# Hybrid encoder step on one core: key transposes queued behind a later token tile, index query weight loaded later

## Chip, cores, metric

The kernel runs on one core of one Trainium2 chip. The metric is the device time of one execution in microseconds, the median of several runs. Times inside the execution are counted from the first instruction of the profiled execution.

## What is computed

One inference step of a one-layer encoder, for 1024 frames of a new stream (eight token tiles of 128 rows) and for 8 x 16 frames of running streams (a ninth token tile). Cut to the part that matters here:

```
h    = rmsnorm(x, norm_mix)              # x: 1152 x 1024
proj = h @ w_in                          # 1024 x 2376, split into:
xr, gate, q, k, v, qi, ki, wi = parts
ki   = rope(ki, pos)                     # index keys, 64 wide, one per token
qi   = rope(qi.reshape(T, 8, 64), pos)   # index queries, 512 columns of w_in
score = sum_h relu(qi_h . ki) * wi_h     # picks 256 keys per query
...                                      # RG-LRU, attention over the picked keys, output, SwiGLU
```

Products are made from pairs of float32r numbers (a rounded part, "hi", and the rest, "lo"), three matmuls for one product.

## The kernel before

The program is written as Python generators, called streams, that emit instructions and yield the time after which they want to go on. `run` (line 93) steps them by a clock of its own, made of planner costs (0.137 us for a projection matmul, 0.109 us for a transpose, and fixed costs of the other engines). It keeps at most `width` main streams open and opens the next when one has ended; `side` streams such as the weight loader are stepped when their own time has come. The order of emission is the priority with which a scheduler then fills each engine's queue at build time; it may bring an instruction forward past earlier ones on its engine. In the first stage TensorE's order in the trace is that of emission, while ScalarE, VectorE and the DMA queue show instructions that were brought forward.

The first stage has nine main streams `norm_kv(i)` (line 555), one for each token tile, with `W_NORM = 3` open at once. One of them, for tile i:

- loads x(i) (512 KB, line 561; the pool has four such buffers);
- `norm_T` (line 466): ScalarE squares and sums a row, VectorE makes the inverse root and scales x(i); then TensorE makes eight 128 x 128 transposes in two groups of four (line 217), and each group is split by ScalarE (hi, 128 x 512) and VectorE (lo, 128 x 512) into the tile `h`;
- 24 matmuls of 328 columns against the weight `wk` give keys, values, index keys and index weights of this tile (line 207);
- ScalarE copies the result to `kv` and squares two 64-column parts of it; the rotary embedding makes the index key `kr` from `kv` (`rope`, VectorE, with two products on POOL from tile 3 on); `kr` goes out by DMA (line 591);
- `stack_keys` (line 596): one transpose of `kr` on TensorE, two ScalarE copies and two VectorE subtractions into the stacked index keys `ki1` and `ki2`.

With three streams open in step, emission comes in groups of three: the x transposes of three tiles, the 72 matmuls of the three, the three `kr` transposes, then the next three tiles. Tile 0 goes first and alone, tiles 1 to 3 follow as a group, then 4 to 6, then 7 and 8. Start times `X_T` hold tiles 0 to 2 apart.

The `loader` (line 420) is a side stream. Its first job is `load_512` (line 608): four DMAs of 512 KB into two `raw` buffers bring the 512 columns of the index query weight; each is split into two weight tiles by a ScalarE copy (hi) and a POOL subtraction (lo, 128 x 512). With `LOAD_AT = 0` the loader begins at once. The next stage, `index` (line 622), starts with tile 8 and needs this weight, `h` and later `ki1`, `ki2`.

After that come the LRU group, attention, the output projection and the feed-forward part, which ends the kernel.

Of the kernel before, what the change touches and what calls it, by code (L numbers as in the profile page):

```python
# [21 lines left out]
NT = 9  # L22
# [59 lines left out]
class Kernel:  # L82
# [131 lines left out]
    def tr(self, out, in_):  # L214
        self.pe += 0.109
        n = in_.shape[0]
        self.nc.tensor.transpose(out, in_, self.ident[0:n, 0:n])  # L217

    def ps(self, n=512, name="ps"):
        return self.psum.tile([128, 512], F32, tag="b", name=name)  # L220
# [45 lines left out]
    def build(self, upto=99):  # L266
# [14 lines left out]
        self.hblk = ctx.enter_context(tc.tile_pool(name="h", bufs=6, side=L))  # L281
        tka_p = pool(tka, "tka", L)
        ki_p = pool(kist, "ki", L)
        self.wused, self.W, self.locks, self.n_norm = 0, {}, set(), 0

        self.ident = self.const.tile([128, 128], F32, name="ident")
        self.eps = self.const.tile([128, 1], F32, name="eps")
# [59 lines left out]
        with tc.tile_pool(name="woa", bufs=2, side=R) as tp:  # L347
            self.phase = 3
            kr, qr = self.k_rope(tp), self.q_norm(tp)
# [55 lines left out]
    LRU_HE = ('pool', 'pool', 'pool', 'pool', 'pool', 'pool', 'pool', 'pool')  # L405
    Q_HE = 'pool'
    W_NORM = 3
    LOAD_AT = 0
    WK_LO = ('dve', 'dve', 'dve', 'dve')
    W_IDX = 4  # L410
    LRU_C = 7
# [8 lines left out]
    def loader(self):  # L420
# [6 lines left out]
        jobs += [(("wb", q, c), 2, lambda n, q=q, c=c: self.load_wb(q, c, n)) for q in range(2) for c in (0, 2)]  # L427
        while self.n_norm < self.LOAD_AT:
            yield 1.0
# [125 lines left out]
    def norm_kv(self, i, tp, g, wk):  # L555
        nc, I, O = self.nc, self.I, self.O
        self.n_norm += 1
        x = self.x.pop(i, None)
        if x is None:
            x = tp.tile([128, D], F32, tag="x", name="x", bufs=4)  # L560
            nc.sync.dma_start(x, self.x_src(i))
        if i < len(self.X_T):
            yield from self.until(self.X_T[i])
        yield from self.norm_T(x, x, g, self.h[i // 3], (i % 3) * 128, tp)
        t = self.ready
        yield 0.0
        yield from self.until(max(t, self.WK_T))
        pk = self.ps()
        for d in range(ND):
            self.mm3(pk[:, :328], self.h_lhs(i, d, 0), self.h_lhs(i, d, 1), wk[:, d, 0, :], wk[:, d, 1, :],  # L570
                     d == 0, d == ND - 1)
        self.begin()
        kv = tp.tile([128, 328], F32, tag="kv", name="kv")
        nc.scalar.activation(kv, pk[:, :328], AF.Copy)
        tab = self.tables(tp, i)
        kr = tp.tile([128, 64], F32, tag="kr", name="kr")
        self.rope(kr[:, None, :], kv[:, None, 256:320], tab, 1, tp, "dve", self.KR_E[i > 2], "dve")
        t = self.end() + self.KV_LAT
        nc.gpsimd.tensor_scalar(self.kn[:, i, :], kv[:, 0:128], 1.0, 0.0, op0=ALU.mult, op1=ALU.add)
        sq = tp.tile([128, 128], F32, tag="sq", name="sq")  # L580
        for a in range(2):
            nc.scalar.activation(sq[:, a * 64:a * 64 + 64], kv[:, a * 64:a * 64 + 64], AF.Square, scale=0.125,
                                 accum_out=self.kss[:, i, a:a + 1])
        self.hi(self.vhl[:, i, 0, :], kv[:, 128:256], "pool")
        self.lo(self.vhl[:, i, 1, :], kv[:, 128:256], self.vhl[:, i, 0, :])
        vo = O["v_p"][0, i * 128:(i + 1) * 128] if i < NP else O["v_s"].rearrange("b t k d -> (b t) k d")
        nc.sync.dma_start(vo.rearrange("t k d -> t (k d)"), kv[:, 128:256])
        nc.gpsimd.tensor_scalar(self.wi[:, i, :], kv[:, 320:328], 8.0 ** -0.5 * 64.0 ** -0.5, 0.0,
                                op0=ALU.mult, op1=ALU.add)
        ko = O["ki_p"][0, i * 128:(i + 1) * 128] if i < NP else O["ki_s"].rearrange("b t d -> (b t) d")  # L590
        nc.sync.dma_start(ko, kr)
        yield 0.0
        yield from self.until(t)
        self.stack_keys(kr, self.ki1[:, i * 128:(i + 1) * 128], self.ki2[:, i * 128:(i + 1) * 128])

    def stack_keys(self, src, k1, k2):

# [442 lines left out]
    def lru_main(self, n, c, lp):  # L1040
# [62 lines left out]
        def gates(t):  # L1103
            xc = xcs[t]
            if not t:
                trs.append(lp.tile([128, 1152], F32, tag="tr", name="tr", bufs=2))
            tr, ti, tt = trs[0][:, 384 * t:384 * t + 384], third("ti"), third("tt")
            G.append((tr, ti, tt))
            for k, dst in ((0, tr), (1, ti)):
                pg = self.ps()  # L1110
                self.mm4(pg[:, :384], bd[:, k, :], xc, True, True)
                S.activation(dst, pg[:, :384], AF.Tanh, scale=0.5, bias=hb[:, c, k:k + 1])
            S.activation(tt, tr, AF.Tanh, scale=sp2[:, c:c + 1], bias=sp2[:, c:c + 1])
            V.scalar_tensor_tensor(ti, ti, 1.0, xc, op0=ALU.add, op1=ALU.mult)
            self.c_free += 1
# [637 lines left out]
```

## Time and profile before

| what | value |
|---|---|
| median of 3 runs | 1537.71 us (1537.52 to 1539.65) |
| the profiled execution's own time | 1536.94 us |
| its span, first to last instruction | 1535.1 us |
| mean granted TensorE clock | 0.98 of full |
| first index matmul on TensorE | 72.59 us |
| TensorE busy | 1467.9 us (96%) |

In rows of a timeline the first number is the start, the second the time from the start of the first to the end of the last instruction of a merged row, then engine, line, operation, output and input tiles, shapes and count; the bracket is the engine's idle time before the row and what ended it. PE is TensorE, DVE VectorE, ACT ScalarE, SPq the queue of the sync engine that issues the DMAs. PEclk is the granted clock, 1.00 for 2.4 GHz and 0.50 for 1.2 GHz.

### The profile page before, as it was taken

The page shows a single profiled execution, that of the slowest core. Times are in us where ns is not written, and L with a number is a line of the kernel's source. Part 1 is how long each engine was busy: PE and PEld are TensorE (multiplying, and loading weights), DVE is VectorE, ACT ScalarE, POOL GpSimd, SP SyncE. Part 2 cuts the span into 40 slices and gives each one's busy share as a digit, 9 for nine tenths or more (in the row PEclk, how much of TensorE's full clock was granted, in tenths as well). Part 3 has the DMA queues.
Part 4 walks back from the last instruction along what each step waited for, and adds up shares of the span by engine and source line. Part 5 has one row for each costly group of instructions (what it writes and reads, how often), then busy time and mean ns, then how long its engine had stood idle before and what let it go on. Part 6 is the DMA issues. An engine that isn't in the chain of part 4 may idle for free.

```text
span 1535.1 us, 20876 instructions
## 1 busy us (share of the span) xinstructions
PE 1467.9 (96%) x7786; PEld 1307.5 (85%) x7786; DVE 865.2 (56%) x1904; ACT 619.2 (40%) x1481; POOL 269.7 (18%) x425
## 2 busy tenths in 40 slices
PE   6889899889997999999999999999999999999998
PEld 6877688778745788889999998989898989898987
DVE  7556899899967988777233333342424242515233
ACT  5447988977415877745202020202121212111100
POOL 4214234333774544300000000000000000000000
PEclk8999899999998999999999999999999999999999
DMA  7201110010401002122102020202021111111003
GB/s 241 58 18 30 48 38 22 12 31 32 176 28 28 1 15 69 28 69 82 56 0 83 0 83 1 83 5 79 18 66 28 56 42 42 50 34 56 28 1 123
DMA packets 95093, 75.24 MB, mean 49 GB/s; under 512 B 13380, under 2 KB 85828, under 8 KB 94992
## 3 DMA queue, kind: packets, MB, share of 16 engines
q1 hardware_dynamic: 94992, 73.91, 15.9%
q8 instruction: 61, 1.00, 0.3%
q14 instruction: 40, 0.33, 0.1%
HBM read 67.62 MB, written 6.27 MB: 48 GB/s over the span
## 4 chain that ended last, share of the span: by engine, by line
PE 72%; DVE 13%; ACT 6%; issue 5%; POOL 2%; DMA 1%; SPq 0%; ACTq 0%; DVEq 0%; POOLq 0%
PE ps L207 66%; DVE junk L66 4%; PE ps L217 3%; ACT jk L66 3%; PE ps L212 3%; DVE tk_cand L66 2%; DVE tr L66 1%; ACT L66 1%; POOL rp L66 1%; DVE ti L66 1%; DVE qn L66 1%; ACT tr L66 1%; DVE m L66 1%; ACT relu L66 1%; DVE s L66 1%
## 5 line engine op out<-in xcount | busy, mean ns | idle before, releaser
L207 PE MATMUL ps<-hf,w 128*128 128x384 f32 x2556 | 453.1, 334 | 0.0
L207 PEld LDWEIGHTS ps<-hf,w 128*128 128x128 f32 x2556 | 444.2, 188 | 0.7
L207 PE MATMUL ps<-w,a 128*128 128x512 f32 x999 | 238.4, 389 | 0.0
L66 DVE TENSOR_TENSOR acc<-ps,acc 128x512 f32<-128x512 f32 x234 | 161.0, 690 | 118.2 <-PE ps L207 117.4
L207 PEld LDWEIGHTS ps<-w,a 128*128 128x128 f32 x999 | 187.3, 188 | 38.5
L66 ACT ACTIVATE w<-raw 128x512 fp32r<-128x512 f32 x124 | 75.2, 628 | 295.7 <-PE ps L207 219.2
L66 DVE TENSOR_TENSOR sg<-ps,sg 128x384 f32<-128x384 f32 x66 | 36.8, 557 | 276.7 <-PE ps L207 276.1
L66 ACT ACTIVATE a<-sg 128x384 fp32r<-128x384 f32 x66 | 34.5, 523 | 219.4 <-DVE sg L66 219.4
L66 DVE TENSOR_TENSOR w<-raw,w 128x512 fp32r<-128x512 f32 x116 | 76.9, 688 | 81.7 <-ACT w L66 81.5
L207 PE MATMUL ps<-hf,rest 128*128 128x384 f32 x612 | 114.3, 334 | 0.0
L66 ACT ACTIVATE jk<-s,tk_cand 128x384 bf16<-128x384 f32 (+3 forms) x128 | 99.5, 777 | 32.4 <-DVE tk_cand L66 29.7
L207 PEld LDWEIGHTS ps<-hf,rest 128*128 128x128 f32 x612 | 106.9, 188 | 0.2
L207 PE MATMUL ps<-h,w 128*128 128x384 f32 x576 | 106.7, 342 | 0.0
L207 PEld LDWEIGHTS ps<-h,w 128*128 128x128 f32 x576 | 100.4, 188 | 3.9 <-ACT relu L66 0.2
L207 PE MATMUL ps<-w,h 128*128 128x256 f32 (+1 forms) x600 | 97.7, 320 | 0.0
L207 PEld LDWEIGHTS ps<-w,h 128*128 128x128 f32 x600 | 85.1, 194 | 6.5
L66 ACT ACTIVATE sg<-ps 128x384 f32<-128x384 f32 x66 | 32.0, 486 | 119.7 <-PE ps L207 119.7
L212 PE MATMUL ps<-wa,yF 128*128 128x512 f32 x144 | 63.4, 593 | 2.4 <-DVE k L66 1.5
L66 POOL TENSOR_SCALAR m<-m,mx 128x128 f32<-128x128 f32 (+7 forms) x64 | 51.7, 814 | 54.1 <-DVE mx L66 45.2
L212 PEld LDWEIGHTS ps<-wa,yF 128*128 128x128 f32 x144 | 26.5, 190 | 35.5 <-issue 31.9
L66 ACT ACTIVATE m<-m,mx 128x128 f32<-128x128 f32 (+7 forms) x64 | 49.3, 771 | 16.4 <-DVE mx L66 16.0
L207 PE MATMUL ps<-k,qeo 128*128 128x384 f32 (+5 forms) x192 | 51.9, 383 | 3.7 <-DVE qeo L66 2.9
(266 smaller groups left out, 2139.8 us busy)
## 6 DMA issues: line engine op xcount, KB each, us to landing
raw<-in_w_ffn_in_dram SPq DMA_DIRECT2D x44, 512.0 KB
raw<-in_w_ffn_out_dram SPq DMA_DIRECT2D x22, 512.0 KB
raw<-in_w_in_dram SPq DMA_DIRECT2D x16, 512.0 KB
out_dram<-acc SPq DMA_DIRECT2D x9, 512.0 KB
x<-in_x_prompt_dram SPq DMA_DIRECT2D x8, 512.0 KB
acc<-in_x_prompt_dram SPq DMA_DIRECT2D x8, 512.0 KB
tab<-in_rope_dram SPq DMA_DIRECT2D x43, 64.0 KB
wa<-in_w_out_dram SPq DMA_DIRECT2D x4, 512.0 KB
```

The costliest lines, as they stand in the source:

```text
L66: return f(*args, **kw)
L207: self.nc.tensor.matmul(out, lhsT, rhs, start=start, stop=stop)
L212: self.nc.tensor.matmul(out, lhsT, rhs, start=start, stop=stop)
L217: self.nc.tensor.transpose(out, in_, self.ident[0:n, 0:n])
```

## The change

Each `norm_kv(i)` notes the last x transpose of its tile. Before `stack_keys`, stream i waits until the x transposes of tile i + 2 (at most tile 8) have been emitted, and the `kr` transpose gets an edge that puts it behind the last of them in TensorE's queue. The loader begins when the fourth `norm_kv` has begun. No instruction is added or removed.

```diff
     def tr(self, out, in_):
         self.pe += 0.109
         n = in_.shape[0]
-        self.nc.tensor.transpose(out, in_, self.ident[0:n, 0:n])
+        self.last_tr = self.nc.tensor.transpose(out, in_, self.ident[0:n, 0:n]).ins
...
-    LOAD_AT = 0
+    LOAD_AT = 4
...
         yield from self.norm_T(x, x, g, self.h[i // 3], (i % 3) * 128, tp)
+        self.xt[i] = self.last_tr
         t = self.ready
...
         yield 0.0
         yield from self.until(t)
-        self.stack_keys(kr, self.ki1[:, i * 128:(i + 1) * 128], self.ki2[:, i * 128:(i + 1) * 128])
+
+        n = min(i + 2, NT - 1)
+        while n not in self.xt:
+            yield 0.3
+        with self.tc.issue_after(self.xt[n]):
+            self.stack_keys(kr, self.ki1[:, i * 128:(i + 1) * 128], self.ki2[:, i * 128:(i + 1) * 128])
```

## Rows read from the trace of the kernel before

**Rows 1.** The page's head: span, TensorE's busy time, and the shares of the chain that ended last, by engine.

```profile
span 1535.1 us, 20876 instructions
PE 1467.9 (96%) x7786; PEld 1307.5 (85%) x7786; DVE 865.2 (56%) x1904; ACT 619.2 (40%) x1481; POOL 269.7 (18%) x425
PE 72%; DVE 13%; ACT 6%; issue 5%; POOL 2%; DMA 1%; SPq 0%; ACTq 0%; DVEq 0%; POOLq 0%
```

**Rows 2.** Busy time by stage, from the view of windows: the window, its length, busy us of TensorE, its weight loads, VectorE, ScalarE and POOL with their instruction counts, granted clock, DMA share, GB/s.

```profile
20.50:31.30 10.80, 5.42 (x25) 5.05 (x26) 9.15 (x21) 7.92 (x20) 5.51 (x8) 0.63 0.55 168
31.30:45.40 14.10, 12.42 (x77) 12.15 (x76) 13.08 (x41) 8.69 (x31) 7.55 (x15) 0.92 0.59 173
...
800.00:1535.00 735.00, 730.63 (x3865) 685.90 (x3863) 262.92 (x414) 121.03 (x225) 0.00 (x0) 1.00 0.15 46
```

**Rows 3.** TensorE's timeline through the first stage.

```profile
19.48 1.02 PE L207 MATMUL ps<-wk,h 128*128 128x328 f32 x5 [0.62 <-DVE nr L66]
24.68 0.42 PE L217 MATMUL ps<-ident,kr 128*64 128x128 f32 x1 [4.18 <-DVE kr L66]
24.89 3.62 PE L217 MATMUL ps<-ident,x 128*128 128x128 f32 x16
29.71 1.94 PE L217 MATMUL ps<-ident,x 128*128 128x128 f32 x8 [1.20 <-DVE x L66]
31.30 12.15 PE L207 MATMUL ps<-wk,h 128*128 128x328 f32 x72
...
45.34 0.27 PE L217 MATMUL ps<-ident,kr 128*64 128x128 f32 x1 [1.68 <-DVE kr L66]
45.45 2.78 PE L217 MATMUL ps<-ident,x 128*128 128x128 f32 x24
47.99 11.10 PE L207 MATMUL ps<-wk,h 128*128 128x328 f32 x72
58.93 0.38 PE L217 MATMUL ps<-ident,kr 128*64 128x128 f32 x2
60.98 0.27 PE L217 MATMUL ps<-ident,kr 128*64 128x128 f32 x1 [1.67 <-DVE kr L66]
61.09 1.91 PE L217 MATMUL ps<-ident,x 128*128 128x128 f32 x16
63.25 7.49 PE L207 MATMUL ps<-wk,h 128*128 128x328 f32 x48 [0.25 <-DVE h L66]
...
72.54 0.30 PE L217 MATMUL ps<-ident,kr 128*64 128x128 f32 x1 [1.69 <-DVE kr L66]
72.59 11.17 PE L207 MATMUL ps<-w,h 128*128 128x512 f32 x48
```

**Rows 4.** The granted clock in windows of 2 us (columns as in rows 2).

```profile
22.00:24.00 2.00, 0.00 (x0) 0.00 (x0) 2.00 (x3) 0.63 (x2) 2.00 (x2) 0.84 0.76 199
...
32.00:34.00 2.00, 2.00 (x10) 2.00 (x10) 1.97 (x4) 2.00 (x6) 1.30 (x2) 0.60 0.86 242
34.00:36.00 2.00, 2.00 (x15) 2.00 (x14) 2.00 (x4) 0.83 (x2) 1.81 (x2) 1.00 0.84 287
```

**Rows 5.** VectorE's timeline in the same stage: the subtractions for `wk`, the scaling of x, the rotary embedding of tile 0, and single rows beside POOL's work.

```profile
10.40 0.84 DVE L66 TENSOR_TENSOR wk<-yF,wk 128x656 fp32r<-128x656 f32 x1 [0.67 <-POOL wk L66]
...
16.75 2.68 DVE L66 TENSOR_TENSOR wk<-yF,wk 128x656 fp32r<-128x656 f32 x2
...
20.61 2.25 DVE L66 SCALAR_TENSOR_TENSOR x<-x,ss,gmix 128x1024 f32<-128x1024 f32 x1
22.78 1.35 DVE L66 TENSOR_TENSOR rp<-kv,tab 128x32 f32<-128x32 f32 x2
...
24.39 0.23 DVE L66 TENSOR_TENSOR kr<-kr,rp 128x64 f32<-128x64 f32 x1
...
33.30 1.28 DVE L66 TENSOR_TENSOR ss<-nr,nr 128x1 f32<-128x1 f32 x1
34.50 0.68 DVE L66 TENSOR_TENSOR h<-ps,h 128x512 fp32r<-128x512 f32 x1
...
37.71 1.28 DVE L66 SCALAR_TENSOR_TENSOR x<-x,ss,gmix 128x1024 f32<-128x1024 f32 x1
```

**Rows 6.** POOL's timeline: the first four and the last two subtractions of the index query weight.

```profile
16.94 7.04 POOL L66 TENSOR_TENSOR w<-raw,w 128x512 fp32r<-128x512 f32 x4
...
33.27 2.54 POOL L66 TENSOR_TENSOR w<-raw,w 128x512 fp32r<-128x512 f32 x2 [0.70 <-ACT w L66]
```

**Rows 7.** ScalarE's timeline: a copy of `kv` and the last of its two squares, and the h copies of tiles 7 and 8.

```profile
40.20 0.44 ACT L66 ACTIVATE kv<-ps 128x328 f32<-128x328 f32 x1 [1.64 <-issue]
...
41.08 0.19 ACT L66 ACTIVATION_READ_ACCUMULATOR sq<-kv 128x1 f32 x1
...
61.87 2.07 ACT L66 ACTIVATE h<-ps 128x512 fp32r<-128x512 f32 x4
```

**Rows 8.** The DMA queue's issues: the first two loads of the index query weight, and the load of x(3).

```profile
10.73 1.18 SPq L455 DMA_DIRECT2D raw<-in_w_in_dram  x2
...
13.07 0.34 SPq L561 DMA_DIRECT2D x<-in_x_prompt_dram  x1
```

More of the change, by code (lines that the diff above doesn't have):

```diff
@@ L283, in build @@
         ki_p = pool(kist, "ki", L)
-        self.wused, self.W, self.locks, self.n_norm = 0, {}, set(), 0
+        self.wused, self.W, self.locks, self.n_norm, self.xt = 0, {}, set(), 0, {}
         self.ident = self.const.tile([128, 128], F32, name="ident")
```

## The prediction

> **What bounds the kernel now.** The page's head comes first: TensorE is busy 96% of the span and holds 72% of the chain that ended last [rows 1]. The windows by stage then say where the missing 4% is. From 800 us to the end TensorE is busy 730.6 of 735 us at full clock [rows 2], so a microsecond won or lost in the first stage is carried to the end, as long as the stages between keep their order. The change touches only the first stage, which ends where the first index matmul starts, at 72.59 us [rows 3].
>
> In that stage the reader is to see two things. TensorE's timeline has gaps in front of index key transposes: 4.18 us before that of tile 0, 1.68 and 1.67 us before the last one of each group of three, 1.69 us before that of tile 8; one of 1.20 us stands before the x transposes of tile 3 [rows 3]. While TensorE waited for `kr` of tile 0, the scaled x(1) lay ready: its sixteen transposes with those of x(2) start at 24.89, directly behind. The second thing is the clock. TensorE falls to 1.2 GHz in the window from 22 to 24 us, in which it did nothing, and is back at 2.4 GHz only in the window after 32 us [rows 4]; the sixteen x transposes took 3.62 us at the low clock and sixteen others 1.91 us at the high one [rows 3]. VectorE is the second bound: it is busy 22.2 of the 24.9 us from 20.5 to 45.4 [rows 2], so what TensorE gives up as waiting may be asked of VectorE next.
>
> **The change, part by part.** *The key transposes.* Nothing is added; nine transposes of about 0.11 us (0.38 us for two against 0.27 us for one [rows 3]) move behind eight x transposes each. For tile 0 that fills the gap: x(1) and x(2) are transposed while `kr` of tile 0 is made. But the code does a second thing. Stream i may not end before x(i+2) is transposed, and only three streams are open, so stream i+3 cannot begin before that either. The groups of three dissolve. A norm takes longer in the planner than a tile's 24 matmuls, so from tile 3 on the emission becomes: matmuls of tile i, x transposes of tile i+1, key transpose of tile i-1, matmuls of tile i+1. The key transpose then comes a whole tile late and waits for nothing: the gaps of 1.68 and 1.67 us go. In exchange each tile's matmuls stand directly behind their own x transposes, and must wait until ScalarE and VectorE have made `h` of them. In groups of three that was hidden: 24 x transposes took until 47.99 us and the matmuls followed with no gap. The one place that shows it nearly alone is tiles 7 and 8: transposes start at 61.09, the matmuls at 63.25, so 2.16 us from start to start [rows 3].
>
> That gives the sum. Tile 0's matmuls end at 20.50 (19.48 + 1.02). Tile 1's can start at 22.7 at the earliest (20.50 + 2.16) and at 25.3 at the latest: `kr` of tile 0 arrives at 24.6 as before [rows 5], and one subtraction for `h` of 0.68 us follows it on VectorE. I take 23.9, because the chain to `kr` holds two `wk` subtractions that took 2.68 us and would take 1.68 at the 0.84 us of the first one [rows 5]; the excess lies where POOL works on the index weight [rows 6]. Tiles 1 and 2 have their transposes done by then: two times 3.70 us (11.10 / 3 [rows 3]) makes 31.3. The clock adds something: at the low clock 72 matmuls took 1.05 us more (12.15 against 11.10). Without the long idle stretch it may stay up, and I take half, 0.5: 31.8. The bounds are 0 and the 1.05. Tiles 3 to 8 cost 3.70 + 2.16 = 5.86 us each, together 35.2: 67.0. The end stays: from tile 8's last matmul (63.25 + 7.49 = 70.74) to the first index matmul at 72.59 are 1.85 us, with the wait for `kr` of tile 8, which has nothing behind which it could be put. The index stage starts at 68.8 instead of 72.59, **3.8 us earlier**.
>
> Of the 2.16 us only 1.04 are TensorE's work (0.93 for eight transposes, 2.78 / 3, and 0.11 for the key), so 1.12 us of each tile stand open. Its bounds are 1.04 (all covered) and 3.89: the ScalarE copy to `kv` and the two squares, 1.07 us from 40.20 to 41.27 [rows 7], stand in front of the h copies, which in the row of 61.87 started 0.78 us after the transposes, so some 0.45 more; and a scaling of x of 1.28 us [rows 5] can lie in front of the subtraction. I stay at 2.16, the only row of that very sequence.
>
> *The later load.* Four DMAs, eight ScalarE copies and eight POOL subtractions are the same as before, with lower priority. In the DMA queue x(3) no longer stands behind two of them (1.18 us of issue [rows 8]). That alone is worth nothing: the 1.20 us in front of x(3) were VectorE's scaling, not its landing. The weight itself is not late: its first load to its last subtraction were some 25 us before (10.73 to 35.81 [rows 6, 8]), and from 24 us on that makes 49, with the index stage at 69. If that cover were gone, each microsecond would be one.
>
> What it can bring is a free VectorE. Beside POOL's subtractions the scaling of x took 2.25 us instead of 1.28, and a one-column operation 1.28 us, while a subtraction that reads PSUM kept its 0.68 us [rows 5, 6]. The Trainium skill ("SBUF — State Buffer", section "SBUF: two separate sides") calls the port pair of VectorE and GpSimd an exclusive lock, under which a VectorE operation with two SBUF inputs is blocked for the whole GpSimd instruction; these rows agree. By that rule the load moves the blocking and removes none of it, which speaks against this half of the change: what tile 0's chain wins, the scaling and rotary embedding of tiles 1 to 4 pay.
>
> No other queue is made to wait: the ScalarE copies into `ki1` and `ki2` come a tile later, and their first readers are in the index stage.
>
> **The sum.** The profiled execution took 1536.94 us, 1.84 us around its span of 1535.1; the median of the runs is 0.77 above it. 1536.94 - 3.8 = 1533.1 for a profiled execution, 1533.9 as a median. About 0.2% (3.1 us) is what a measurement of this kernel can tell from no change.
>
> **Rivals.** *Cover found:* the scheduler brings the next tile's x transposes forward into the open 1.12 us. For it: VectorE's scalings run ahead of TensorE. Against: in the trace x(4) to x(6) stayed behind the key transpose of tile 3, though TensorE waited 1.68 us. Six times 1.12 us more, 1527.2.
>
> *VectorE takes over:* the scheduler brings the weight's loads forward anyway, since the DMA queue and POOL have room at 12 to 20 us, and POOL blocks VectorE in the same place. For it: rows 2 and the lock. Then tile 1 starts at 25.3 (1.4 lost), and one contended scaling (0.97 more) lands in front of a tile's `h`: a gain of 1.4, 1536.3.
>
> *The open evacuation is longer (slower):* from tile 3 on the matmuls wait for ScalarE's squares (0.45 us) and for part of a scaling on VectorE (0.8 of 1.28): 3.4 us from transposes to matmuls. Six times 1.24 us is 7.4, the gain of 3.8 turns to a loss of 3.6, 1541.3. It decides from 2.16 + 3.8 / 6 = 2.8 us on. For it: VectorE's 93% to 45.4 us. Against: it has room later, and has the whole of a tile's matmuls for the scaling.
>
> *It does nothing:* the emission is later than planned but the queues come out the same, 1537.7.
>
> **How the numbers follow.** Forecast 0.45, cover 0.10, VectorE 0.25, longer evacuation 0.13, nothing 0.07. The forecast's own spread, 22.7 to 25.3 for tile 1's start and the clock's 0.5 either way, leaves 0.09 of its 0.45 within 0.2%; VectorE's case gives 0.04 to faster. So faster 0.50, same 0.37, slower 0.13. The range goes from 1529.5, past the forecast's bounds and partly to the cover, to 1539.5, over the VectorE case, no change, and the near half of the loss.
>
> **What would show it.** Right: x transposes of tiles 1 and 2 ahead of the first key transpose, no `kr` wait but those of tiles 0 and 8, matmuls in 24s each about 2.2 us behind their transposes, full clock before 28 us, and the first index matmul near 69 us. Wrong: an idle time <-DVE h above 1.8 us a tile, a first stage of 72 us or more, tile 1's matmuls after 25.5, or a shift at the stage's end that the later stages give back.

## The result and the profile after

| | before | changed |
|---|---|---|
| median | 1537.71 us | 1528.2 us (1527.1 to 1534.16, 5 runs) |
| ratio to before | | 0.995 (0.9937 to 0.9963) |
| the profiled execution, its span | 1536.94, 1535.1 us | 1534.16, 1532.3 us |
| mean granted clock | 0.980 | 0.979 |
| first index matmul on TensorE | 72.59 us | 65.06 us |

The change makes the kernel faster by 0.5%, 7.7 us by the ratio (5.7 to 9.7). The forecast was 3.8 us, a median of 1533.9 in a range from 1529.5 to 1539.5. The ratio applied to the median of before gives 1530.0, inside that range; the bare median, 1528.2, lies 1.3 us below its lower end. So about twice the forecast gain came, at the edge of the range. The profiled execution of the changed kernel is the slowest of its five, so its span shows only 2.8 us of the gain; what it lost again, it lost after the first stage (last section). The first stage itself reads clearly. This is TensorE's timeline of the changed kernel, to be laid beside [rows 3]:

```profile
14.92 1.97 PE L217 MATMUL ps<-ident,x 128*128 128x128 f32 x8
16.54 2.07 PE L207 MATMUL ps<-wk,h 128*128 128x328 f32 x11
19.16 1.09 PE L217 MATMUL ps<-ident,x 128*128 128x128 f32 x8 [0.56 <-DVE x L66]
22.30 0.27 PE L217 MATMUL ps<-ident,kr 128*64 128x128 f32 x1 [2.04 <-DVE nr L66]
22.33 7.21 PE L207 MATMUL ps<-wk,h 128*128 128x328 f32 x36
...
32.08 2.06 PE L207 MATMUL ps<-wk,h 128*128 128x328 f32 x12
...
35.68 0.30 PE L217 MATMUL ps<-ident,kr 128*64 128x128 f32 x1 [0.67 <-DVE kr L66]
37.66 5.27 PE L207 MATMUL ps<-wk,h 128*128 128x328 f32 x24 [1.69 <-DVE h L66]
...
45.48 2.05 PE L207 MATMUL ps<-wk,h 128*128 128x328 f32 x12
47.37 1.03 PE L217 MATMUL ps<-ident,x 128*128 128x128 f32 x8
48.16 2.05 PE L207 MATMUL ps<-wk,h 128*128 128x328 f32 x12
50.05 0.28 PE L217 MATMUL ps<-ident,kr 128*64 128x128 f32 x1
50.08 2.06 PE L207 MATMUL ps<-wk,h 128*128 128x328 f32 x12
...
59.28 3.86 PE L207 MATMUL ps<-wk,h 128*128 128x328 f32 x24
62.98 0.27 PE L217 MATMUL ps<-ident,kr 128*64 128x128 f32 x1
65.04 0.27 PE L217 MATMUL ps<-ident,kr 128*64 128x128 f32 x1 [1.78 <-DVE kr L66]
65.06 11.17 PE L207 MATMUL ps<-w,h 128*128 128x512 f32 x48
```

The reader is to see where the x transposes stand. Those of x(1) lie inside tile 0's matmuls (14.92, between the first 13 and the last 11). From 45 us on each tile up to tile 7 is 12 matmuls, x transposes of the next tile, 12 matmuls, and the key transpose of the tile before (in tile 6 two of the eight x transposes come behind its last matmuls): tile 5 starts at 45.48, tile 6 at 50.08, tile 8 at 59.28, so 4.60 us a tile with no wait at all. The windows of this trace (columns as in rows 2) show the same: from 45.4 to 59.3 us TensorE is never idle, and before that VectorE is the fuller engine.

```profile
20.30:29.40 9.10, 7.10 (x38) 7.11 (x39) 8.88 (x21) 6.59 (x19) 6.54 (x7) 0.81 0.69 200
29.40:45.40 16.00, 13.64 (x87) 13.17 (x86) 14.57 (x45) 11.00 (x35) 10.81 (x15) 0.89 0.56 159
45.40:59.30 13.90, 13.90 (x103) 13.76 (x101) 9.20 (x23) 8.11 (x28) 4.16 (x15) 1.00 0.14 38
```

The waits that are left before 45 us, 2.04, 0.67 and 1.69 us, have POOL's subtractions of the index query weight beside them. POOL's timeline of the changed kernel, then VectorE's:

```profile
18.98 2.51 POOL L66 TENSOR_TENSOR w<-raw,w 128x512 fp32r<-128x512 f32 x2 [3.52 <-ACT w L66]
...
31.40 3.51 POOL L66 TENSOR_TENSOR w<-raw,w 128x512 fp32r<-128x512 f32 x2 [1.20 <-ACT w L66]
```

```profile
19.79 1.75 DVE L66 TENSOR_TENSOR rp<-kv,tab 128x32 f32<-128x32 f32 x2
...
31.44 2.33 DVE L66 SCALAR_TENSOR_TENSOR x<-x,ss,gmix 128x1024 f32<-128x1024 f32 x1
33.69 1.24 DVE L66 SCALAR_TENSOR_TENSOR nr<-nr,nr 128x1 f32<-128x1 f32 x1
```

The two `rp` products of tile 0's key take 1.75 us instead of the 0.38 that the same pair takes later in this trace, the scaling 2.33 instead of 1.28, one column 1.24 instead of 0.2.

### The profile page after: what moved, and what is told of

The parts are those of the page before. It is cut to its first block, busy times and chain, and to the rows that moved or that the text cites. A ratio compares the mean times of both kernels' runs of the same rounds, so it can differ in the third digit from the quotient of the medians.

```text
span 1532.3 us, 20880 instructions
## 1 busy us (share of the span) xinstructions
PE 1471.5 (96%) x7786; PEld 1309.0 (85%) x7786; DVE 867.1 (57%) x1904; ACT 618.5 (40%) x1481; POOL 266.2 (17%) x425
## 4 chain that ended last, share of the span: by engine, by line
PE 73%; DVE 11%; ACT 9%; issue 4%; POOL 3%; DMA 1%; SPq 0%; ACTq 0%; POOLq 0%; DVEq 0%
PE ps L207 66%; PE ps L217 3%; ACT jk L66 3%; DVE junk L66 3%; PE ps L212 3%; DVE tk_cand L66 2%; DVE tr L66 1%; ACT tr L66 1%; POOL rp L66 1%; ACT L66 1%; ACT relu L66 1%; DVE m L66 1%; DVE ti L66 1%; POOL s L66 0%; DMA acc<-in_x_prompt_dram 0%
## 5 line engine op out<-in xcount | busy, mean ns | idle before, releaser
L207 PE MATMUL ps<-smr,vhl 128*128 128x512 f32 x162 | 55.0, 425 | 2.4 <-ACT smr L66 1.9
```

Source lines behind the costliest of these rows:

```text
L207: self.nc.tensor.matmul(out, lhsT, rhs, start=start, stop=stop)
```

## The experiments

Two theories stood against each other at first. Theory A: the changed order of emission lets the scheduler bring the next tile's x transposes in between the matmuls of a tile, and the stage is TensorE's work alone from then on. Theory B: the later load frees VectorE, and the key transposes matter little. Of the first four kernels, two have one half of the change each, one has it whole, and one has it without the scheduler's freedom.

**e1, the later load alone.**

```diff
 (kernel before)
-    LOAD_AT = 0
+    LOAD_AT = 4
```

> The kernel before with LOAD_AT = 4 alone; key transposes as before. Theory A (the gain is TensorE's new order: the x transposes of the next tile come next in emission and are brought into the matmuls of the tile ahead): the groups of three and their gaps of about 1.7 us stay, only the head gains, first index matmul at 69 to 71 us, median 1534 to 1536. Theory B (the freed VectorE at the head is what counts): first index matmul near 66, median near 1529.

Measured: 1537.37 us beside 1538.24, ratio 0.999 (0.998 to 1.0). From 45 us on TensorE's timeline keeps the groups of three, and the waits for `kr` stay:

```profile
24.08 0.42 PE L217 MATMUL ps<-ident,kr 128*64 128x128 f32 x1 [3.24 <-DVE kr L66]
...
31.22 1.04 PE L217 MATMUL ps<-ident,x 128*128 128x128 f32 x8
...
45.11 0.27 PE L217 MATMUL ps<-ident,kr 128*64 128x128 f32 x1 [3.09 <-DVE kr L66]
45.22 2.78 PE L217 MATMUL ps<-ident,x 128*128 128x128 f32 x24
...
72.37 8.00 PE L207 MATMUL ps<-w,h 128*128 128x512 f32 x34
```

The first key waits 3.24 us instead of 4.18 [rows 3], and the key that ends the next group waits 3.09 instead of 1.68: what VectorE won in front, the group took back. By itself the load is worth 0.2 us at the first index matmul, less than theory A expected (69 to 71 us). In the first group x transposes do stand between the matmuls (31.22), in the old emission too; those of the next three tiles (45.22) stay behind the key transpose.

**e2, the key transposes alone.**

```diff
 (changed kernel)
-    LOAD_AT = 4
+    LOAD_AT = 0
```

> The changed kernel with LOAD_AT = 0: key transposes behind the token tile two later, weight load from the start. Theory A: first index matmul at 66 to 68, median 1529 to 1532, most of the gain. Theory B: 71 to 73, median within 2 us of before.

Measured: 1535.69 us beside 1538.24, ratio 0.999 (0.9979 to 1.0). This misses theory A (66 to 68 us, 1529 to 1532) and lies near theory B's numbers. The x transposes do slide in between the matmuls, and from 46.83 us on a tile costs 4.6 us as in the changed kernel. But TensorE runs into VectorE before that, beside four of POOL's subtractions in one piece from 19.37 to 25.38 us and two more pairs from 33.17 and 38.55 us:

```profile
23.02 1.97 PE L217 MATMUL ps<-ident,x 128*128 128x128 f32 x8 [2.08 <-DVE x L66]
...
25.91 9.21 PE L207 MATMUL ps<-wk,h 128*128 128x328 f32 x48
...
39.07 2.88 PE L207 MATMUL ps<-wk,h 128*128 128x328 f32 x12 [2.96 <-DVE h L66]
...
70.95 9.33 PE L207 MATMUL ps<-w,h 128*128 128x512 f32 x40
```

So neither half gives the gain. Together they give 0.5%, where the two ratios multiplied would give 0.2%: the new order makes VectorE's time count, and the later load thins out what POOL takes from it at the head. The distance to e3 below, 3.35 us at the first index matmul (70.95 - 67.60), fits this: tile 1 starts 1.66 us later (25.91 against 24.25), behind a scaling of x(2) that took 2.25 us beside POOL instead of 1.28, and its matmuls run at a lower clock (48 in 9.21 us, where e3's pace would give 7.56).

**e3, the changed kernel unaltered**, as the measure for the others.

> The changed kernel once more, unaltered, to see how far its runs spread and what of the first profile belongs to that one execution. First index matmul 64 to 66.5; median 1527 to 1531, single executions 1527 to 1534. If the spread comes from TensorE's low clock in the later stages, two profiles differ there and not in the order of instructions.

Measured: 1529.4 us, ratio 0.9947 (0.9931 to 0.9963). Its order is the same as in the first profile; the first index matmul is at 67.60 us, with a second wait for `h` (1.65 and 1.54 us). That is later than expected, and two of the six executions took longer than the expected 1534 us (1536.19 and 1535.76).

```profile
24.25 5.67 PE L207 MATMUL ps<-wk,h 128*128 128x328 f32 x36
```

One profile of this kernel is therefore good to some 2.5 us in the first stage.

**e4, the changed kernel with the freedom taken away.**

```diff
 (changed kernel; last_mm is the matmul emitted last)
+    if xs is x and self.n_norm > 3:
+        st.enter_context(self.tc.issue_after(self.last_mm))
     for j in range(4):
         self.tr(pt[:, j * 128:(j + 1) * 128], ...)
```

> The changed kernel with the x transposes of tiles 3 to 8 queued behind the last matmul of the tile ahead: the order that the prediction took for the changed kernel. Theory A: six tiles lay open the time in which h is made, about 1.1 us each, 6 to 7 us later than the changed kernel: first index matmul at 71 to 73, median 1534 to 1537, waits of TensorE for DVE h of about 1.1 us a tile. Theory B (the order in the steady part does not matter): first index matmul within 1.5 us of the changed kernel.

Measured: 1540.39 us beside 1538.24, ratio 1.0014 (1.0006 to 1.0023), some 11 us above e3 and later than expected (71 to 73 us, 1534 to 1537). TensorE's timeline:

```profile
36.53 3.43 PE L207 MATMUL ps<-wk,h 128*128 128x328 f32 x12 [3.21 <-DVE h L66]
...
51.44 3.87 PE L207 MATMUL ps<-wk,h 128*128 128x328 f32 x24 [2.10 <-DVE h L66]
55.14 1.04 PE L217 MATMUL ps<-ident,x 128*128 128x128 f32 x8
56.02 0.27 PE L217 MATMUL ps<-ident,kr 128*64 128x128 f32 x1
57.41 3.87 PE L207 MATMUL ps<-wk,h 128*128 128x328 f32 x24 [1.12 <-DVE h L66]
...
74.92 5.27 PE L207 MATMUL ps<-w,h 128*128 128x512 f32 x22
```

This is the order that the forecast assumed, and its price: 5.97 us for each of tiles 5 to 7 (57.41 - 51.44 for tile 5), with 1.12 us open, but 7.93 and 6.98 us for tiles 3 and 4 (36.53 to 44.46 to 51.44). There the waits for `h` are 3.21 us in front of tile 3, with a low clock behind (12 matmuls in 3.43 us instead of 2.06), and 2.10 in front of tile 5. What theory A says of the order is shown: without the freedom the whole change is a small loss (0.06 to 0.23%). Its other half, that TensorE's work alone is left, falls with e2, and theory B falls with e1.

**e5, the edge taken out, the wait of the stream kept.**

```diff
 (changed kernel)
-        with self.tc.issue_after(self.xt[n]):
-            self.stack_keys(kr, ...)
+        self.stack_keys(kr, ...)
```

> The edge that puts each key transpose behind the x transposes of tile i + 2 is taken out; the wait of the stream (the later place in the order of emission) stays. Theory A, the emission alone frees the order: TensorE's order and the time stay those of the changed kernel, first index matmul at 65 to 68 us, 1528 to 1531 us. Rival, the edge is what holds the key transpose back: the scheduler brings it forward, the waits of 2 to 4 us in front of key transposes return, first index matmul at 70 us or later, 1533 us or more.

Measured: 1530.77 us beside 1536.61, ratio 0.995 (0.9934 to 0.9967); first index matmul at 67.20 us, the rows of TensorE in the same sequence. The edge does nothing; the later place in the emission does it all.

**e7, only tile 0's key transpose moved**, the later load kept.

```diff
 (changed kernel)
-        n = min(i + 2, NT - 1)
+        n = min(i + 2, NT - 1) if i == 0 else i
```

> The changed kernel, but only tile 0's key transpose waits for the x transposes of tile 2; those of tiles 1 to 8 are emitted as before the change, the later load is kept. Theory A, each group's key waits count too: the gap of 4.18 us before tile 0's key closes, but waits <-DVE kr of 1.6 to 1.8 us come back behind the later groups, first index matmul 2 to 4 us later than with the whole change (68 to 70 us), 1531 to 1534 us. Rival, the whole gain is tile 0's gap and the shorter low clock: 1528 to 1530 us.

Measured: 1533.84 us beside 1536.61, ratio 0.9986 (0.9972 to 1.0001), about a quarter of the gain. The start is that of the changed kernel (the 36 matmuls of tile 1 and half of tile 2 begin at 22.71 us), then the key waits come back, from 45 us on with the groups:

```profile
59.64 0.27 PE L217 MATMUL ps<-ident,kr 128*64 128x128 f32 x1 [1.67 <-DVE kr L66]
...
71.25 9.14 PE L207 MATMUL ps<-w,h 128*128 128x512 f32 x39
```

The first index matmul came later than expected (71.25 against 68 to 70). The gap that looks largest in the profile of before, 4.18 us, is not where most of the gain is.

**e6 and e8, POOL's subtractions put later.** Theory L: the waits that the change leaves stand where POOL's subtractions lie beside a scaling that TensorE needs soon. In e6 two of them follow POOL's last operation of each of tiles 3 to 6, in e8 of tiles 4 to 7 (`4 + q`).

```diff
 (changed kernel, load_512; wi_last[i] is POOL's last operation of tile i)
-                self.split(w, t[:, o, :], "act", "pool")
+                self.hi(w[:, 0], t[:, o, :], "act")
+                while 3 + q not in self.wi_last:
+                    yield 0.3
+                with self.tc.issue_after(self.wi_last[3 + q]):
+                    self.lo(w[:, 1], t[:, o, :], w[:, 0], "pool")
                 out.append(w)
-                yield 2.0
+                yield 0.3
```

> The changed kernel, with POOL's eight subtractions of the index query weight put behind POOL's own last operation of tiles 3 to 6, two behind each, so after 43 us instead of between 19 and 39 us. Theory L, POOL's subtractions hold VectorE up (x scaling 2.3 instead of 1.3 us, one-column operations 1.2 instead of 0.15 us) just where TensorE waits for h: the waits <-DVE h near 35 to 41 us (1.69 us in one profile, 1.65 + 1.54 in another) go, the first index matmul starts 1.5 to 3 us earlier (62 to 66 us), 1525 to 1527.5 us. Rival R1, the waits are VectorE's own work (14.6 of 16 us busy): they stay, 1528 to 1530 us. Rival R2, the weight or tile 4 to 7's h comes late now: TensorE waits <-POOL w or <-DVE h after 45 us, 1530 us or more.

Measured for e6: 1528.72 us beside 1536.61, ratio 0.9946 (0.9933 to 0.996). TensorE's timeline, then POOL's and VectorE's:

```profile
22.19 0.27 PE L217 MATMUL ps<-ident,kr 128*64 128x128 f32 x1 [0.49 <-DVE kr L66]
...
42.40 2.48 PE L207 MATMUL ps<-wk,h 128*128 128x328 f32 x12 [2.51 <-DVE h L66]
...
63.53 11.14 PE L207 MATMUL ps<-w,h 128*128 128x512 f32 x48
```

```profile
38.15 2.52 POOL L66 TENSOR_TENSOR w<-raw,w 128x512 fp32r<-128x512 f32 x2
```

```profile
21.22 0.39 DVE L66 TENSOR_TENSOR rp<-kv,tab 128x32 f32<-128x32 f32 x2
...
34.22 1.28 DVE L66 SCALAR_TENSOR_TENSOR x<-x,ss,gmix 128x1024 f32<-128x1024 f32 x1
...
39.49 2.26 DVE L66 SCALAR_TENSOR_TENSOR x<-x,ss,gmix 128x1024 f32<-128x1024 f32 x1
```

Without POOL beside it, tile 0's `rp` takes 0.39 us and its key waits 0.49 instead of 2.04; no wait for `h` is left up to 39 us. Then POOL's first pair lies beside a scaling, which takes 2.26 us, and a new wait of 2.51 us stands behind it. The wait went where POOL's work went. Theory L holds as to place; the time, 1528.72, is within the noise of the changed kernel's, so the expected 1525 to 1527.5 was missed.

> As the run before with POOL's subtractions put later, but one tile later still: two behind POOL's last operation of each of tiles 4 to 7 (from 43 us on). Theory L, a wait for h arises where POOL's subtractions fall beside a scaling of x that TensorE needs soon: the wait of 2.51 us <-DVE h at 42.4 us and the low clock from 43.6 us go, x scalings stay at 1.3 us to 42 us, the first index matmul starts at 59 to 61.5 us, 1523.5 to 1527 us. Rival R1, TensorE overtakes VectorE there in any case: a wait of 1 us or more for h stays near 40 to 45 us, 63 to 64 us, 1527.5 to 1530 us. Rival R2, the last weight parts come too late: a wait <-POOL w at the first index matmuls, 1528 us or more.

Measured for e8: 1528.38 us beside 1538.08, ratio 0.9929 (0.9916 to 0.9941). TensorE's timeline:

```profile
40.39 2.07 PE L207 MATMUL ps<-wk,h 128*128 128x328 f32 x12 [0.90 <-DVE h L66]
...
46.11 2.08 PE L207 MATMUL ps<-wk,h 128*128 128x328 f32 x12 [0.86 <-DVE h L66]
...
61.35 0.27 PE L217 MATMUL ps<-ident,kr 128*64 128x128 f32 x1 [1.78 <-DVE kr L66]
61.38 11.16 PE L207 MATMUL ps<-w,h 128*128 128x512 f32 x48
```

The wait of 2.51 us became 0.90 and 0.86, and no <-POOL w appears, although the last pair of the weight ended at 60.2 us, just ahead of the first index matmul. That matmul came as expected, 3.7 us before that of the changed kernel's first profile; the median did not (1523.5 to 1527 was expected). POOL still holds VectorE up, here at the low part of the values, which no matmul of this stage reads. POOL's first pair, then VectorE beside it:

```profile
41.40 2.52 POOL L66 TENSOR_TENSOR w<-raw,w 128x512 fp32r<-128x512 f32 x2
```

```profile
42.69 1.38 DVE L66 TENSOR_TENSOR vhl<-kv,vhl 128x128 fp32r<-128x128 f32 x1
```

Away from POOL's subtractions this operation takes 0.28 us in the same trace. The scalings of x keep 1.28 or 1.29 us.

**e9, the same late subtractions (tiles 4 to 7) in the kernel before**, with `LOAD_AT = 4` and the key transposes where they were.

> The kernel before the change, its key transposes where they were, with POOL's eight subtractions of the index query weight put behind its last operation of tiles 4 to 7, and the loader begun at the fourth tile. Theory A, the order of TensorE bounds the stage and the freed VectorE is worth only the first gap: tile 0's kr comes some 2 us earlier, the waits of 1.6 to 3 us <-DVE kr before the other key transposes stay, first index matmul at 68.5 to 71 us, 1533 to 1536 us. Rival, POOL's hold on VectorE was the whole bound and the key transposes only showed it: first index matmul at 65 to 67.5 us, 1528 to 1531 us.

Measured: 1535.9 us beside 1538.08, ratio 0.9982 (0.997 to 0.9993).

```profile
40.69 0.39 PE L217 MATMUL ps<-ident,kr 128*64 128x128 f32 x1 [3.00 <-DVE kr L66]
...
70.66 9.57 PE L207 MATMUL ps<-w,h 128*128 128x512 f32 x41
```

A free VectorE is worth 1.9 us at the first index matmul in the old order, with key waits up to 3.00 us, and 3.7 to 6.2 us in the new one (61.38 against 65.06 and 67.60). Order first, then VectorE.

**e10 and e11, the last version and the changed kernel on one chip.**

> The kernel with POOL's subtractions behind tiles 4 to 7 once more, now beside the changed kernel on the same chip. Its first index matmul came at 61.4 us, 3.7 to 6.2 us before that of the changed kernel's profiles (65.1 to 67.6). Theory K, the first stage's gain is kept to the end: 1524 to 1527 us, 2 to 5 us under the changed kernel. Rival, the stages after it give it back by their low clock: within 1.5 us of the changed kernel, 1527 to 1530 us.

> The changed kernel, unaltered, beside the one with POOL's subtractions later. Both theories: 1527.5 to 1531 us; first index matmul at 65 to 68 us. What is asked is its distance to the other kernel: 2 to 5 us by theory K, under 1.5 us by the rival.

Measured: 1526.48 us, ratio 0.9928 (0.9911 to 0.9944), beside 1528.4 us, ratio 0.995 (0.9932 to 0.9968), and 1538.61 for before. The first index matmul came at 61.13 and 64.97 us. The medians lie 1.9 us apart, between the two theories (2 to 5, under 1.5), and the intervals overlap: the later subtractions beat the kernel before, and probably the changed one (0.9929 and 0.9928 against 0.9947 to 0.995), which these runs do not settle.

Set side by side, the first stage's shift and the time of the runs go together to within some 3 us: where the first index matmul moved by -7.6 to -5.0 us (the changed kernel and e5, four profiles) the ratio gives -8.2 to -7.7 us, by -11.5 and -11.2 (e8, e10) -11, by -9.1 (e6) -8.3, by -1.9 (e9) -2.8, by -1.6 (e2) -1.5, by -1.3 (e7) -2.2, by -0.2 (e1) -1.5, by +2.3 (e4) +2.2.

## Why the prediction was right in direction and too small

**What failed: the order.** The step "from tile 3 on the emission becomes: matmuls of tile i, x transposes of tile i+1 ..., each tile's matmuls stand directly behind their own x transposes", at 5.86 us a tile, was wrong. It was the rival "cover found", given a chance of 0.10, that came true for tiles 5 to 7, with 4.60 us a tile: 3.70 of matmuls and 0.90 of transposes. The reason set against it, that x(4) to x(6) had stayed behind the key transpose of tile 3 in the trace of before, was read as a limit of the scheduler, while it was one of that emission: there the key transposes came next in the emission, so the x transposes would have had to pass them. In the changed kernel the next tile's x transposes come next and need to pass only matmuls. That x transposes do pass matmuls, e4 shows by forbidding it, and e1's first group shows it in the old emission; that the place of the key transposes in the emission decides, e1, e5 and e7 show. The scheduler's own rule is only argued.

**The price was right for three tiles of six.** e4 has the assumed order and costs 5.97 us with 1.12 us open for tiles 5 to 7, against 5.86 and 1.12. For tiles 3 and 4 it costs 7.93 and 6.98, and tile 3's matmuls start at 36.53 us where the forecast's terms give 33.96. So the assumed order puts the first index matmul at 74.92 us instead of the forecast 68.8, a loss and not a gain. That the direction came true was luck as far as the mechanism goes: it came by another order.

**The sum, term by term**, in the changed kernel's profile. Tile 1 starts at 22.33 us there, and at 23.65, 24.25 and 24.50 in e11, e3 and e5; forecast 23.9 (22.7 to 25.3; the step named there, 25.3 less the 1.00 us of the two `wk` subtractions, gives 24.3). The reason given holds: the two `wk` subtractions took 1.58 us, tile 0's key still comes late on VectorE, and the gap before it, 4.18 us, shrank to 2.04, with x(1)'s transposes moved into tile 0's matmuls and x(2)'s into the gap. Tile 3's matmuls start at 32.08, where the forecast had tiles 1 and 2 end at 31.8. Tiles 3 and 4 then cost 6.70 us each (45.48 - 32.08 over two) instead of 5.86, tiles 5 to 7 4.60, tile 8 3.70 (62.98 - 59.28), and the end 2.08 instead of 1.85. 0.28 + 2 x 0.84 - 3 x 1.26 - 2.16 + 0.23 = -3.75, which is 65.06 against 68.8.

**VectorE as the next bound** was the rival with 0.25, and half of it is there: the scheduler did bring the weight's first loads forward, and the waits of 0.67 and 1.69 us, with a low clock behind them (0.89 in 29.4 to 45.4), are VectorE's beside POOL. The load that the program begins only with the fourth `norm_kv` was issued just 0.89 us later on the chip (11.62 us against 10.73), and POOL's first subtraction started 2.04 us later (18.98 against 16.94). That hold on VectorE cost tiles 3 and 4 what the sum above shows, not the whole gain; 1.40 us of that is the clock (the 24 matmuls at 37.66 took 5.27 us, the same row in e11 at the full clock 3.87).

**POOL's hold on VectorE.** In e6 a scaling of x takes 2.26 us beside POOL's pair and 1.28 away from it, and the wait moves with the pair. The Trainium skill ("SBUF — State Buffer", section "SBUF: two separate sides") has VectorE and GpSimd share one port pair as an exclusive lock; these runs agree with it. The prediction took from it that the load moves the blocking and removes none: so it was in e6. What it missed is that the place can be chosen: e8 moved all eight subtractions behind POOL's last operation of tile 4, and the stage came out 3.7 to 6.2 us shorter.

**The clock.** The forecast gave 0.5 us for a shorter low clock. In the windows the clock is 0.81 and 0.89 of full up to 45.4 us; the 36 matmuls from 22.33 took 7.21 us, and in e3, where the same row has the full clock, 5.67. It gained little in the first profile. The clock goes with the waits: from 20 to 45 us it was 0.80 in before and in e2, 0.86 and 0.93 in the changed kernel (the first profile and e3), and 1.00 in e8, where no wait in that stretch was longer than 0.90 us. Part of what the runs above gain or lose with a wait is the clock behind it; no run separates the two.

**The longer evacuation**, the slower rival, needed the strict order. In e4 the waits for `h` of 3.21 and 2.10 us are there, and it did come out slower than before. So of the two outcomes under the assumed order the forecast took the wrong one as the likelier (0.45 against 0.13).

**The rest** held: the edge cost nothing (e5), no wait for the moved copies of `ki1` and `ki2` appears on TensorE, the index weight was never late, and the wait before tile 8's key stayed (1.78 us). One sign named for being wrong, a shift that the later stages give back, stands in the first profile (7.5 us at the end of the stage, 2.8 at the end) and not in e11's.

## What to carry to other kernels

Before pricing a moved instruction, ask what it stood in the way of: here the scheduler filled gaps with x transposes where they had only matmuls to pass, and not where a key transpose came next in the emission. An order read from one trace holds for that emission alone, so price the new order both ways, strict and filled, and give them chances from what separates them. Two edits in one stage can be worth little apart and much together, when the first only moves the bound to an engine that the second relieves.

## What the runs showed that was not expected

The same kernel with the same order takes 1526.84 us in one profiled execution (e11) and 1534.16 in another (the first), though the first index matmul stands at 64.97 and 65.06 us. The difference arises between 330 and 720 us. The windows of that stretch, in the first profile and then in e11's (columns as in rows 2):

```profile
330.00:720.00 390.00, 364.14 (x1953) 289.49 (x1952) 318.01 (x801) 234.76 (x634) 154.75 (x222) 0.96 0.16 49
```

```profile
330.00:720.00 390.00, 366.06 (x2005) 291.90 (x2005) 320.70 (x811) 239.47 (x642) 154.94 (x222) 0.98 0.17 52
```

TensorE is busy for nearly as long in both (366.06 and 364.14 us), but at a granted clock of 0.98 it gets through 52 more matmuls than at 0.96. So the lead of 7.5 us over the profiled execution of the kernel before shrank to 2.8 at the end of the one execution (spans 1532.3 and 1535.1) and grew to 10.2 in the other (1524.9). Why the clock falls more often in one execution than in another stays open; the effect of a change of a few microseconds has to be read from the stage and from many runs, not from two profiles.
